# First MLP product by seven block products, with weight sums formed in SBUF by DVE and by transfers

## The chip, the cores and the metric

One core of one Trainium2 chip runs the whole kernel; there is one launch. The metric is the device time of that launch in microseconds, as the median of several executions. Lower is better.

## The reference, cut to what matters

One decoder layer on 256 tokens of width 2048, in fp32. The part that the change rewrites is the first MLP product; all else (attention heads, pooling, output projection, final norm) is computed as before.

```python
z = rmsnorm(h, norm2_w) @ mlp_w1          # [256, 2048] @ [2048, 8192]
h = h + jnp.square(jax.nn.relu(z)) @ mlp_w2   # [256, 8192] @ [8192, 2048]
h = rmsnorm(h, final_norm_w)
```

## The kernel before

Every product is made of matmuls on fp32r operands (a rounded fp32 form of TensorE). To keep fp32 accuracy an operand is split into a rounded part `hi` and a remainder `lo`, and three matmuls (hi·hi, hi·lo, lo·hi) stand for one product. The activations are split once and stay in SBUF. The weights are streamed: `wts` holds them as chunks of [128, 2048] floats (1 MB) in the order of their use. `raw_chunk` (L92) loads a chunk by a DMA on SP's queue into one of three `raw` buffers. `halves` (L99) splits it in two halves of 1024 columns: ScalarE copies to `hi` (L75), VectorE subtracts to `lo` (L76). There are four `hi` and four `lo` buffers, so splitting can run four halves ahead of TensorE and no further.

`as_chunk` (L208) multiplies one chunk with both token tiles (t = 0, 1, of 128 tokens): four k-tiles, two token tiles, three matmuls of 128x512, so 24 matmuls a chunk and 12 a half. After each half it calls `run_side`, which pops one piece of side work (transposes, evacuations) from the list `side` and issues it there.

The MLP runs in eight groups of 1024 hidden columns. `mlp1(g)` (L671) makes the hidden columns of group g: two strips of 512 columns, four chunks each, 192 matmuls; ScalarE and VectorE form relu² of them (L683, L685), and `back` transposes the result on TensorE (`turn4`, L635) and splits it into `z_hi`, `z_lo`. `mlp2(g)` (L697) multiplies these with the second weight matrix, 8 chunks and 192 matmuls, and `add_h` (L627) adds the sums to `h`. The loop runs `mlp1(g)` and then `mlp2(g - 1)` for g = 1 to 7; `mlp1(0)` stands ahead of it, and the second product of group 7 is the tail, one token tile after the other.

Ahead of `mlp1(0)`, the output projection (L651) fills `h`, and `make_u2` (L638) transposes it to `u2_hi`, `u2_lo`; these transposes wait in `side` and ride in the chunks that follow. The norm's factor is applied to the hidden columns, as a per-token scale (L683). The final norm's weights `fw` are loaded and scaled early (L611, L615).

A scheduler orders the instructions of every engine ahead of time; at run time each engine takes its queue strictly in order, and SP issues the loads in order.

Of the kernel before, what the change touches and what calls it, by code (L numbers as in the profile page):

```python
# [36 lines left out]
def hybrid_gla_pool_kernel(  # L37
# [17 lines left out]
    cp = ctx.enter_context(tc.tile_pool(name="cp", bufs=1))  # L55
    big = ctx.enter_context(tc.tile_pool(name="big", bufs=1))
# [4 lines left out]
    accp = ctx.enter_context(tc.tile_pool(name="accp", bufs=4, space=PSUM))  # L61
    gpp = ctx.enter_context(tc.tile_pool(name="gpp", bufs=4, space=PSUM))
    gt = ctx.enter_context(tc.tile_pool(name="gt", bufs=4))
    gstack = ctx.enter_context(ExitStack())
    gq = gstack.enter_context(tc.tile_pool(name="gq", bufs=1))

    def acc():
        return accp.tile([P, 512], F32, tag="acc", name="acc")
# [3 lines left out]

    # ---------------------------------------------------------------- weights
    def split(raw, hi, lo):
# [69 lines left out]

    # ------------------------------------------------------------- 1 / rms
    def rsqrt(dst, ssq, n, parts, w):
# [168 lines left out]

    # log gates over natural tokens (the factor 1/16 sits in the triangles)
    lgs = []
# [25 lines left out]

    # ke: meta tokens to their end, tile 0 to its end, the first chunk of each tile to its end
    def gates(h, t):
# [41 lines left out]

    # values
    vn = [gq.tile([P if t < 2 else META, H * DV], F32, tag=f"vn{t}", name=f"vn{t}") for t in range(3)]
# [22 lines left out]

    # queries
    qd = [gq.tile([P, S], F32, name=f"qd{h}") for h in range(H)]
# [83 lines left out]

    # output gate
    for s in range(2):  # L500
# [36 lines left out]

    # multi-scale pooling
    mo = []
# [53 lines left out]
    for g in range(4):  # L593
        p = ws_next(META - (2 << g))
        if g == 3:
            while side:
                side.pop(0)()
        side[1:1] = pooling(g, p)

    gstack.close()  # L600

    # ================================================================ phase 2
    lp = ctx.enter_context(tc.tile_pool(name="lp", bufs=1))
    zt = ctx.enter_context(tc.tile_pool(name="zt", bufs=3))
# [3 lines left out]
    fw = lp.tile([P, D], F32, name="fw")  # L608

    def load_fw():  # L610
        nc.sync.dma_start(out=fw, in_=rows[:, 768 : 768 + D].partition_broadcast(P))  # L611

    def scale_fw():
        # the last rsqrt leaves a factor -8192, a power of two
        dve.tensor_scalar(out=fw, in0=fw, scalar1=-1.0 / 8192.0, scalar2=None, op0=ALU.mult)  # L615

# [4 lines left out]
    rs3 = cp.tile([P, NT], F32, name="rs3")  # L621
    u2_hi = big.tile([P, KD, S], F32R, tag="u_hi", name="u2_hi")
    u2_lo = big.tile([P, KD, S], F32R, tag="u_lo", name="u2_lo")

# [13 lines left out]
    def make_u2(s, t):  # L638
        ps = turn4(h[:, t, s * 512 : (s + 1) * 512])
        ts = slice(t * P, (t + 1) * P)  # L640
        for j in range(4):
            k = 4 * s + j
            pj = ps[:, j * P : (j + 1) * P]
            act.activation(u2_hi[:, k, ts], pj, AF.Copy, scale=n2[:, k : k + 1])
            dve.scalar_tensor_tensor(
                out=u2_lo[:, k, ts], in0=pj, scalar=n2[:, k : k + 1],
                in1=u2_hi[:, k, ts].bitcast(F32), op0=ALU.mult, op1=ALU.subtract,
            )
# [17 lines left out]
    rsqrt(rs2, tot, D, P, NT)  # L666
    dve.tensor_tensor(out=rs2, in0=rs2, in1=rs2, op=ALU.mult)

    rz = {}

    def mlp1(g):  # L671
        nonlocal ci
        z_hi = mp.tile([P, 8, S], F32R, tag="m", name="z_hi")
        z_lo = mp.tile([P, 8, S], F32R, tag="m", name="z_lo")
        rz[g] = (z_hi, z_lo)
        for s in range(2):
            ps = [acc(), acc()]
            for c in range(4):
                as_chunk(ps, ci, u2_hi, u2_lo, 0, 4, 4 * c, c == 0, c == 3)
                ci += 1  # L680
            for t in range(NT):
                r = zt.tile([P, 512], F32, tag="r", name="r")
                act.activation(r, ps[t], AF.Relu, scale=rs2[:, t : t + 1])  # L683
                q = zt.tile([P, 512], F32, tag="q", name="q")
                dve.scalar_tensor_tensor(  # L685
                    out=q, in0=ps[t], scalar=0.0, in1=r, op0=ALU.max, op1=ALU.mult
                )


                def back(s=s, t=t, q=q):  # L690
                    pv = turn4(q).rearrange("p (j c) -> p j c", c=P)
                    ts = slice(t * P, (t + 1) * P)
                    evac_hl(z_hi[:, 4 * s : 4 * s + 4, ts], z_lo[:, 4 * s : 4 * s + 4, ts], pv)

                side.append(back)

    def mlp2(g):  # L697
        nonlocal ci
        z_hi, z_lo = rz.pop(g)
        for s in range(4):  # L700
            ps = [acc(), acc()]
            for c in range(2):
                as_chunk(ps, ci, z_hi, z_lo, 0, 4, 4 * c, c == 0, c == 1)
                ci += 1
            for t in range(NT):
                add_h(ps[t], t, s * 512, (s + 1) * 512)

    mlp1(0)
    side += [load_fw, idle, idle, idle, scale_fw]
    for g in range(1, GROUPS):  # L710
        mlp1(g)
        mlp2(g - 1)
    # ======================================= last group: one token tile after the other
    z_hi, z_lo = rz.pop(GROUPS - 1)
    e_hi = big.tile([P, KD, S], F32R, tag="u_hi", name="e_hi").rearrange("p k c -> p (k c)")
    e_lo = big.tile([P, KD, S], F32R, tag="u_lo", name="e_lo").rearrange("p k c -> p (k c)")
# [34 lines left out]
    for s in range(4):  # L751
        ws = []
        for c in range(2):
            raw = raw_chunk(ci)
            ci += 1
            if s == 2:
                for hf in range(2):
                    o = c * 2048 + hf * 1024
                    hi, lo = e_hi[:, o : o + 1024], e_lo[:, o : o + 1024]
# [29 lines left out]
def _weights(np, w_in, w_out, w1, w2):  # L789
    """All weights as one run of chunks [128, 2048], in the order in which they are used."""  # L790
    def ws(a):  # [2048, n*256] -> n strips of two chunks, each 8 k-tiles of 256 columns
        n = a.shape[1] // 256
        b = a.reshape(2, 8, P, n, 256).transpose(3, 0, 2, 1, 4)
        return b.reshape(n * 2, P, 2048)

    def st(a):  # [512*c, n*512] -> [n, c] chunks, each 4 k-tiles of 512 columns
        c, n = a.shape[0] // 512, a.shape[1] // 512
        b = a.reshape(c, 4, P, n, 512).transpose(3, 0, 2, 1, 4)
        return b.reshape(n, c, P, 2048)
# [16 lines left out]
    for g in range(1, GROUPS):  # L816
        m1(g)
        m2(g - 1)
# [58 lines left out]
```

## Time and profile before

| | |
|---|---|
| median of 3 runs (lowest, highest) | 1049.33 us (1048.45, 1050.74) |
| span of the profiled execution | 1046.9 us |
| TensorE matmuls busy | 1035.2 us, 99% of the span |
| VectorE (DVE) busy | 605.9 us, 58% |
| ScalarE (ACT) busy | 480.6 us, 46% |
| GpSimd (POOL) busy | 0.2 us |
| moved by DMA | 197.15 MB, 188 GB/s over the span |
| granted TensorE clock, mean | 0.997 |

The profile shows one execution. Its page gives the span, from the first instruction to the last, and no further time of that execution; the median of the runs lies 2.4 us above the span. Engine times overlap, so they do not add up. The rows that the prediction uses stand in groups below.

### The profile page before, as it was taken

The page shows a single profiled execution, that of the slowest core. Times are in us where ns is not written, and L with a number is a line of the kernel's source. Part 1 is how long each engine was busy: PE and PEld are TensorE (multiplying, and loading weights), DVE is VectorE, ACT ScalarE, POOL GpSimd, SP SyncE. Part 2 cuts the span into 40 slices and gives each one's busy share as a digit, 9 for nine tenths or more (in the row PEclk, how much of TensorE's full clock was granted, in tenths as well). Part 3 has the DMA queues.
Part 4 walks back from the last instruction along what each step waited for, and adds up shares of the span by engine and source line. Part 5 has one row for each costly group of instructions (what it writes and reads, how often), then busy time and mean ns, then how long its engine had stood idle before and what let it go on. Part 6 is the DMA issues. An engine that isn't in the chain of part 4 may idle for free.

```text
span 1046.9 us, 12935 instructions
## 1 busy us (share of the span) xinstructions
PE 1035.2 (99%) x5237; PEld 877.2 (84%) x5237; DVE 605.9 (58%) x773; ACT 480.6 (46%) x630; POOL 0.2 (0%) x4
## 2 busy tenths in 40 slices
PE   8999999999999999999999999999999999999996
PEld 7989878998888888888888888888888888888885
DVE  7555544876666555555555555565555555555574
ACT  6537544444555444434434433443443344344351
POOL 0000000000000000000000000000000000000000
PEclk9999999999999999999999999999999999999998
DMA  9663434447554545555555555555555555545542
GB/s 348 241 239 137 161 124 159 146 155 288 186 190 172 201 173 189 198 184 182 201 189 179 196 194 184 185 200 186 182 197 191 185 188 199 185 178 201 188 174 81
DMA packets 29820, 197.15 MB, mean 188 GB/s; under 512 B 3456, under 2 KB 3968, under 8 KB 6704
## 3 DMA queue, kind: packets, MB, share of 16 engines
q1 hardware_dynamic: 29760, 196.32, 52.9%
q8 instruction: 41, 0.67, 0.3%
q14 instruction: 19, 0.16, 0.0%
HBM read 194.21 MB, written 2.10 MB: 188 GB/s over the span
## 4 chain that ended last, share of the span: by engine, by line
PE 98%; DMA 1%; SPq 0%; DVE 0%; ACT 0%; issue 0%; ACTq 0%
PE acc L217 25%; PE acc L219 25%; PE acc L218 25%; PE acc L202 4%; PE acc L203 4%; PE acc L204 4%; PE gp L635 2%; PE acc L777 1%; PE acc L776 1%; PE acc L778 1%; DMA raw<-in_wts 1%; PE acc L256 1%; PE acc L258 1%; PE acc L257 1%; PE gp L472 0%; PE gp L473 0%
## 5 line engine op out<-in xcount | busy, mean ns | idle before, releaser
L76 DVE TENSOR_TENSOR lo<-raw,hi 128x1024 fp32r<-128x1024 f32 (+1 forms) x356 | 425.8, 1200 | 373.6 <-ACT hi L75 373.3
L75 ACT CAST hi<-raw 128x1024 fp32r<-128x1024 f32 (+1 forms) x356 | 366.1, 1033 | 484.2 <-PE acc L219 409.4
L217 PE MATMUL acc<-hi,u_hi 128*128 128x512 f32 x576 | 228.5, 397 | 0.0
L219 PE MATMUL acc<-hi,u_lo 128*128 128x512 f32 x576 | 224.8, 390 | 0.0
L218 PE MATMUL acc<-lo,u_hi 128*128 128x512 f32 x576 | 224.5, 390 | 0.0
L217 PE MATMUL acc<-hi,z_hi 128*128 128x512 f32 x448 | 175.7, 392 | 0.0
L219 PE MATMUL acc<-hi,z_lo 128*128 128x512 f32 x448 | 174.5, 389 | 0.0
L218 PE MATMUL acc<-lo,z_hi 128*128 128x512 f32 x448 | 174.4, 389 | 0.0
L219 PEld LDWEIGHTS acc<-hi,u_lo 128*128 128x128 f32 x576 | 108.1, 188 | 23.0
L217 PEld LDWEIGHTS acc<-hi,u_hi 128*128 128x128 f32 x576 | 108.2, 188 | 22.0
L218 PEld LDWEIGHTS acc<-lo,u_hi 128*128 128x128 f32 x576 | 108.3, 188 | 21.7
L219 PEld LDWEIGHTS acc<-hi,z_lo 128*128 128x128 f32 x448 | 84.1, 188 | 17.7
L217 PEld LDWEIGHTS acc<-hi,z_hi 128*128 128x128 f32 x448 | 84.1, 188 | 17.1
L218 PEld LDWEIGHTS acc<-lo,z_hi 128*128 128x128 f32 x448 | 84.2, 188 | 17.0
L202 PE MATMUL acc<-u_hi,hi 128*128 128x272 f32 (+4 forms) x320 | 92.7, 290 | 0.0
L203 PE MATMUL acc<-u_lo,hi 128*128 128x272 f32 (+4 forms) x320 | 91.4, 286 | 0.0
L204 PE MATMUL acc<-u_hi,lo 128*128 128x272 f32 (+4 forms) x320 | 91.2, 285 | 0.0
L202 PEld LDWEIGHTS acc<-u_hi,hi 128*128 128x128 f32 x320 | 60.3, 189 | 1.0 <-issue 0.8
L203 PEld LDWEIGHTS acc<-u_lo,hi 128*128 128x128 f32 x320 | 60.2, 188 | 0.1
L204 PEld LDWEIGHTS acc<-u_hi,lo 128*128 128x128 f32 x320 | 60.1, 188 | 0.0
L627 DVE TENSOR_TENSOR h<-acc,h 128x512 f32<-128x512 f32 (+1 forms) x71 | 45.6, 679 | 5.2 <-PE acc L778 5.2
L683 ACT ACTIVATE r<-acc,rs 128x512 f32<-128x512 f32 x32 | 21.9, 690 | 15.7 <-PE acc L219 15.7
(189 smaller groups left out, 841.6 us busy)
## 6 DMA issues: line engine op xcount, KB each, us to landing
raw<-in_wts SPq DMA_DIRECT2D x175, 1024.0 KB, 4.8
xn<-in_x SPq DMA_DIRECT2D x2, 1024.0 KB, 11.8
h<-in_x SPq DMA_DIRECT2D x2, 1024.0 KB, 6.7
out<-h SPq DMA_DIRECT2D x8, 256.0 KB, 2.9
xTs<-in_xT SPq DMA_DIRECT2D x3, 546.0 KB, 9.7
pw<-in_pool_w SPq DMA_DIRECT2D x4, 256.0 KB, 5.1
fw<-in_rows SPq DMA_DIRECT2D x1, 1024.0 KB, 7.7
raw<-in_wts SPq DMA_DIRECT2D x2, 256.0 KB, 3.5
```

The costliest lines, as they stand in the source:

```text
L75: act.copy(out=hi, in_=raw)
L76: dve.tensor_tensor(out=lo, in0=raw, in1=hi.bitcast(F32), op=ALU.subtract)
L202: pe.matmul(o, hi[:, cs], u_hi[:, k, lo_t:L], start=k == 0, stop=False)
L203: pe.matmul(o, hi[:, cs], u_lo[:, k, lo_t:L], start=False, stop=False)
L204: pe.matmul(o, lo[:, cs], u_hi[:, k, lo_t:L], start=False, stop=k == KD - 1)
L217: pe.matmul(ps[t], a_hi[:, k, ts], hi[:, cs], start=st, stop=False)
L218: pe.matmul(ps[t], a_hi[:, k, ts], lo[:, cs], start=False, stop=False)
L219: pe.matmul(ps[t], a_lo[:, k, ts], hi[:, cs], start=False, stop=sp)
L256: pe.matmul(o, hi[:, cs], u_hi[:, k, :], start=k == 0, stop=False)
L627: dve.tensor_tensor(out=hs, in0=p, in1=hs, op=ALU.add)
L635: pe.transpose(ps[:, j * P : (j + 1) * P], src[:, j * P : (j + 1) * P], ident)
L683: act.activation(r, ps[t], AF.Relu, scale=rs2[:, t : t + 1])
```

## The change

The first product of groups 1 to 7 is computed block by block. For a group, the token tiles (2) times the two halves of the 2048 input channels (2) form four activation blocks, and the input halves times the two strips of 512 columns form four weight blocks. Seven products of sums of such blocks (a Strassen form) replace eight plain block products. Each of the seven is one token tile wide: `product` makes 24 matmuls of 128x512 on two chunks.

- The seven activation operands are made once, during `mlp1(0)`, by `prepare`: the norm's factor is multiplied in (`rms2_rows`, `norm_a`), blocks are added or subtracted (`combine`), and each operand is split to `ah`, `al` and kept in SBUF (pool `asp`).
- The weight sums are made for each group in place. A group loads eight chunks of the first matrix: x (2 chunks), z (2), y (2), v (2). x is used plain in product 1; then `add_load` adds the z block to it by a DMA from GpSimd's queue that accumulates in SBUF, and product 5 uses the sum. The same way y is added to the z tiles, for product 7. `add_raw` adds y and later v to the x tiles on VectorE (128x2048), for products 6 and 4. The chunks of z and y that `add_load` reads come from HBM a second time.
- The chunks of `mlp2(g - 1)` alternate with the products, one `half(j)` of 24 matmuls after each product or so.
- PSUM sums of the products are kept (`keep`, a copy on ScalarE) and combined in `hidden`; relu and square are two ScalarE steps.
- Buffers: four `raw` buffers, and four more of the same size (`xy`), which first hold `u2`. PSUM pools are cut anew after `mlp1(0)`. The side list is emptied ahead of `mlp1(0)`. `fw` is loaded and scaled at the start of the tail. A smaller SBUF area is reserved for GpSimd's DMA descriptors.

```diff
-    rawp = ctx.enter_context(tc.tile_pool(name="rawp", bufs=3))
+    rawp = ctx.enter_context(tc.tile_pool(name="rawp", bufs=4))
...
     rsqrt(rs2, tot, D, P, NT)
...
+    while side:
+        side.pop(0)()
+    gstack.close()
+    asp = ctx.enter_context(tc.tile_pool(name="asp", bufs=1))
...
+    def norm_a(kh):
+        a = mp.tile([P, 8, S], F32, tag="m", name="a")
+        full.append(a)
+        u_h, u_l = (u.bitcast(F32) for u in u2[kh])
+        dve.tensor_tensor(out=a, in0=u_h, in1=u_l, op=ALU.add)
+        dve.tensor_tensor(out=a, in0=a, in1=rb2.unsqueeze(1).to_broadcast([P, 8, S]), op=ALU.mult)
...
+    def operand(i, t, kh, sign=1.0):
+        a = blk(t, kh)
+        hi, lo = (asp.tile([P, 8, P], F32R, name=f"{n}{i}") for n in ("ah", "al"))
+        if sign > 0:
+            act.copy(out=hi, in_=a)
+            dve.tensor_tensor(out=lo, in0=a, in1=hi.bitcast(F32), op=ALU.subtract)
...
+        return [
+            rms2_rows, lambda: norm_a(0), lambda: operand(1, 0, 0), lambda: norm_a(1),
+            lambda: operand(2, 0, 1), s5, s7, s6, s3,
+        ]
...
+    def product(i, ps, raws, start):
+        a_hi, a_lo = ops_a[i]
+        for c in range(2):
+            for hf, (hi, lo) in enumerate(halves(raws[c])):
+                for j in range(2):
+                    k = c * 4 + hf * 2 + j
+                    cs = slice(j * 512, (j + 1) * 512)
+                    kw = dict(skip_group_check=True)
+                    pe.matmul(ps, a_hi[:, k], hi[:, cs], start=start and k == 0, stop=False, **kw)
+                    pe.matmul(ps, a_hi[:, k], lo[:, cs], start=False, stop=False, **kw)
+                    pe.matmul(ps, a_lo[:, k], hi[:, cs], start=False, stop=k == 7, **kw)
+            run_side()
+
+    def add_raw(dst, src):
+        dve.tensor_tensor(out=dst, in0=dst, in1=src, op=ALU.add)
+
+    def add_load(dst, c):
+        nc.gpsimd.dma_start(out=dst, in_=wts[c], accum_op=ALU.add)
...
+        xs = [xy_load(base), xy_load(base + 1)]
+        zs = [xy_load(base + 2), xy_load(base + 3)]
+        product(1, b_a, xs, True)
+        x1 = keep(b_a, "x1")
+        for i in range(2):
+            add_load(xs[i], base + 2 + i)
+        half(0)
+        ys = [raw_chunk(base + 4), raw_chunk(base + 5)]
+        for i in range(2):
+            add_load(zs[i], base + 4 + i)
+        product(5, b_d, xs, True)
+        x5 = keep(b_d, "x5")
+        add_raw(xs[0], ys[0])
+        half(1)
+        add_raw(xs[1], ys[1])
+        product(3, b_d, ys, False)
+        half(2)
+        half(3)
+        product(6, b_a, xs, False)
+        x2 = keep(b_a, "x2")
+        hidden(g, 1, 0, b_d, x2, -1.0)
+        vs = [raw_chunk(base + 6), raw_chunk(base + 7)]
+        add_raw(xs[0], vs[0])
+        half(4)
+        add_raw(xs[1], vs[1])
+        product(7, b_a, zs, False)
+        hidden(g, 1, 1, b_a, x5, -1.0)
+        half(5)
+        product(4, b_a, xs, False)
+        hidden(g, 0, 1, b_a, None, 1.0)
+        half(6)
+        product(2, b_b, vs, True)
+        hidden(g, 0, 0, b_b, x1, 1.0)
+        half(7)
...
+    fw = mp.tile([P, D], F32, tag="m", name="fw")
+    nc.sync.dma_start(out=fw, in_=rows[:, 768 : 768 + D].partition_broadcast(P))
+
+    dve.tensor_scalar(out=fw, in0=fw, scalar1=-1.0 / 8192.0, scalar2=None, op0=ALU.mult)
```

Two places show how the order of the engines' queues changes. A row of an order is: line, operation, written tile <- read tiles, shape, and in brackets the semaphores that it waits for (DMAHW for SP's transfers, DMASW for GpSimd's).

VectorE's queue in the middle of a group, before: `lo` is a split, `h` the add of a finished strip, `z_lo` the evacuation of a transpose.

```order
L76 TENSOR_TENSOR lo_4378<-raw_4375,hi_4377 128x1024 [waits DMAHW5_49,Activation_49]
L685 SCALAR_TENSOR_TENSOR q_4319<-acc_4179,r_4317 128x512 [waits Activation_49]
L685 SCALAR_TENSOR_TENSOR q_4323<-acc_4180,r_4321 128x512 [waits Activation_49]
L76 TENSOR_TENSOR lo_4382<-raw_4375,hi_4381 128x1024 [waits PE_49,Activation_49]
L76 TENSOR_TENSOR lo_4412<-raw_4409,hi_4411 128x1024 [waits DMAHW6_49,Activation_49]
L497 TENSOR_TENSOR z_lo_4178<-gp_4349,z_hi_4177 128x4x128 [waits Activation_49]
L76 TENSOR_TENSOR lo_4416<-raw_4409,hi_4415 128x1024 [waits Activation_49]
```

The same queue now, from the end of product 1 to the first split of half(1) and on; `blk_4940` and `blk_4942` are the two x chunks, `raw_5028` and `raw_5030` the two y chunks.

```order
L621 TENSOR_TENSOR h_2510<-acc_4804,h_2510 128x512 [waits PE_49]
L621 TENSOR_TENSOR h_2510<-acc_4805,h_2510 128x512 [waits PE_49]
L77 TENSOR_TENSOR lo_4973<-blk_4942,hi_4972 128x1024 [waits DVE_49,Activation_49]
L77 TENSOR_TENSOR lo_4997<-raw_4994,hi_4996 128x1024 [waits DMAHW3_49,DVE_49,Activation_49]
L77 TENSOR_TENSOR lo_5001<-raw_4994,hi_5000 128x1024 [waits Activation_49]
L77 TENSOR_TENSOR lo_5035<-blk_4940,hi_5034 128x1024 [waits DMASW2_49,Activation_49]
L77 TENSOR_TENSOR lo_5039<-blk_4940,hi_5038 128x1024 [waits PE_49,Activation_49]
L784 TENSOR_TENSOR blk_4940<-blk_4940,raw_5028 128x2048 [waits DMAHW4_49,DVE_49]
L77 TENSOR_TENSOR lo_5055<-blk_4942,hi_5054 128x1024 [waits DMASW3_49,Activation_49]
L77 TENSOR_TENSOR lo_5059<-blk_4942,hi_5058 128x1024 [waits Activation_49]
L784 TENSOR_TENSOR blk_4942<-blk_4942,raw_5030 128x2048 [waits DMAHW5_49,DVE_49]
L77 TENSOR_TENSOR lo_5080<-raw_5077,hi_5079 128x1024 [waits DMAHW6_49,Activation_49]
```

Two splits wait for GpSimd's transfers (DMASW2, DMASW3), and two adds of 128x2048 stand among the splits.

TensorE's queue where `mlp1(0)` begins, before: `u2` is the transposed `h`, `gp<-cst,h` one block of four transposes of `make_u2`.

```order
L217 MATMUL acc_3220<-hi_3223,u2_hi_2511 128x512
L218 MATMUL acc_3220<-lo_3224,u2_hi_2511 128x512
L219 MATMUL acc_3220<-hi_3223,u2_lo_2512 128x512
L635 MATMUL gp_3243<-cst_85,h_2502 128x128 [waits DVE_49]
L217 MATMUL acc_3219<-hi_3227,u2_hi_2511 128x512 [waits Activation_49]
```

The same place now.

```order
L220 MATMUL acc_3041<-hi_3176,mo_lo_2116 128x512
L218 MATMUL acc_3260<-hi_3264,u2_2518 128x512 [waits Activation_49]
L219 MATMUL acc_3260<-lo_3265,u2_2518 128x512 [waits DVE_49]
L629 MATMUL gp_3228<-cst_85,h_2510 128x128 [waits DVE_49]
L220 MATMUL acc_3260<-hi_3264,u2_2519 128x512
L629 MATMUL gp_3241<-cst_85,h_2510 128x128 [waits DVE_49]
L218 MATMUL acc_3261<-hi_3264,u2_2518 128x512
```

The last transposes of `h` stood after the first half chunk (12 matmuls) and now stand after two matmuls.

## Rows read from the trace of the kernel before

**Rows 1.** The page: busy us, share of the span, instructions of each engine.
```profile
PE 1035.2 (99%) x5237; PEld 877.2 (84%) x5237; DVE 605.9 (58%) x773; ACT 480.6 (46%) x630; POOL 0.2 (0%) x4
```
**Rows 2.** The page: the chain that ended last, shares by engine.
```profile
PE 98%; DMA 1%; SPq 0%; DVE 0%; ACT 0%; issue 0%; ACTq 0%
```
**Rows 3.** Stretches of one group each: length, busy per engine, clock, DMA, GB/s.
```profile
662.93:751.90 88.97, 88.97 (x402) 73.66 (x401) 49.14 (x49) 38.18 (x40) 0.00 (x0) 1.00 0.55 190
751.90:840.87 88.97, 88.97 (x402) 73.66 (x401) 49.13 (x49) 38.18 (x40) 0.00 (x0) 1.00 0.54 189
```
**Rows 4.** Timeline of TensorE in a group: start us, duration us, instruction.
```profile
639.63 0.39 PE L217 MATMUL acc<-hi,u_hi 128*128 128x512 f32 x1
639.86 0.39 PE L218 MATMUL acc<-lo,u_hi 128*128 128x512 f32 x1
...
642.36 0.39 PE L217 MATMUL acc<-hi,u_hi 128*128 128x512 f32 x1
```
**Rows 5.** Waits: engine, line, waited for: us in total, times, longest.
```profile
ACT hi L75 <- PE acc L219: 409.4, 251, 2.7
DVE lo L76 <- ACT hi L75: 373.3, 308, 2.7
```
**Rows 6.** Groups by line and shape: count, busy us, mean ns, idle before.
```profile
L76 DVE TENSOR_TENSOR lo<-raw,hi 128x1024 fp32r<-128x1024 f32 x340 | 415.7, 1224 | 370.8 <-ACT hi L75 370.6
L75 ACT CAST hi<-raw 128x1024 fp32r<-128x1024 f32 x340 | 357.1, 1052 | 481.6 <-PE acc L219 409.4 <-PE acc L203 55.0 <-issue 13.4
L685 DVE SCALAR_TENSOR_TENSOR q<-acc,r 128x512 f32<-128x512 f32 x32 | 21.9, 691 | 7.2 <-ACT r L683 7.2
L683 ACT ACTIVATE r<-acc,rs 128x512 f32<-128x512 f32 x32 | 21.9, 690 | 15.7 <-PE acc L219 15.7
L630 ACT ACTIVATE junk<-h 128x512 f32<-128x512 f32 x14 | 8.7, 626 | 8.8 <-DVE h L627 8.8
L76 DVE TENSOR_TENSOR lg<-lg 128x1536 fp32r<-128x1536 f32 x1 | 1.8, 1758 | 0.4 <-ACT lg L75 0.4
L615 DVE TENSOR_SCALAR fw<-fw 128x2048 f32<-128x2048 f32 x1 | 1.2, 1222 | 0.0
```
**Rows 7.** Timeline of VectorE in the tail, where it runs without a pause.
```profile
1002.30 1.23 DVE L76 TENSOR_TENSOR lo<-raw,hi 128x1024 fp32r<-128x1024 f32 x1 [0.32 <-ACT hi L75]
1003.44 1.22 DVE L76 TENSOR_TENSOR e_lo<-raw,e_hi 128x1024 fp32r<-128x1024 f32 x1
1004.58 1.22 DVE L76 TENSOR_TENSOR lo<-raw,hi 128x1024 fp32r<-128x1024 f32 x1
```
**Rows 8.** Timeline of VectorE at the end of the output projection.
```profile
301.96 1.28 DVE L627 TENSOR_TENSOR h<-acc,h 128x512 f32<-128x512 f32 x2
```
**Rows 9.** DMA issues: tile<-tensor, queue, count, KB each, median us to landing.
```profile
raw<-in_wts SPq DMA_DIRECT2D x175, 1024.0 KB, 4.8
xn<-in_x SPq DMA_DIRECT2D x2, 1024.0 KB, 11.8
fw<-in_rows SPq DMA_DIRECT2D x1, 1024.0 KB, 7.7
```
**Rows 10.** The first loads and the last stretch, columns as in rows 3.
```profile
5.00:15.00 10.00, 8.52 (x60) 7.77 (x59) 6.83 (x14) 6.89 (x14) 0.00 (x0) 1.00 1.00 395
...
1030.00:1047.00 17.00, 8.16 (x59) 7.57 (x57) 7.41 (x26) 3.91 (x8) 0.00 (x0) 0.80 0.34 123
```
**Rows 11.** The chain in order of time: where the last `h` transposes ran.
```profile
305.10 0.44 PE gp L635 x4
308.29 0.44 PE gp L635 x4
```

More of the change, by code (lines that the diff above doesn't have):

```diff
@@ L697, in mlp2 @@
[L697 to L709, printed above, removed]
+    rs2q = cp.tile([P, NT], F32, name="rs2q")
+    dve.tensor_tensor(out=rs2q, in0=rs2, in1=rs2, op=ALU.mult)
@@ new lines, in hybrid_gla_pool_kernel, with rms2_rows @@
+    rb2 = cp.tile([P, S], F32, name="rb2")
+    while side:
+        side.pop(0)()
+    gstack.close()
+    asp = ctx.enter_context(tc.tile_pool(name="asp", bufs=1))
+    def rms2_rows():
+        ps = gp()
+        for t in range(NT):
+            dg = zt.tile([P, P], F32, tag="q", name="dg2")
+            dve.tensor_scalar(out=dg, in0=ident, scalar1=rs2[:, t : t + 1], scalar2=None, op0=ALU.mult)
+            pe.matmul(ps[:, t * P : (t + 1) * P], cst[:, C_ONE : C_ONE + P], dg, start=True, stop=True)
+        dve.tensor_copy(out=rb2, in_=ps[:, :S])
@@ new lines, in combine, with prepare, s5, s7 @@
+    def combine(dst, x0, x1, op):
+        dve.tensor_tensor(out=blk(*dst), in0=blk(*x0), in1=blk(*x1), op=op)
+    def prepare():
+        def s5():
+            operand(4, 1, 1)
+            combine((1, 1), (1, 1), (1, 0), ALU.subtract)
+            operand(5, 1, 1)
+        def s7():
+            combine((1, 0), (0, 0), (1, 0), ALU.subtract)
+            operand(7, 1, 0)
+        def s6():
+            combine((0, 0), (0, 0), (1, 1), ALU.add)
+            operand(6, 0, 0, -1.0)
+        def s3():
+            combine((0, 1), (0, 0), (0, 1), ALU.subtract)
+            operand(3, 0, 1)
+        return [
+            rms2_rows, lambda: norm_a(0), lambda: operand(1, 0, 0), lambda: norm_a(1),
+            lambda: operand(2, 0, 1), s5, s7, s6, s3,
+        ]
@@ new lines, in hybrid_gla_pool_kernel, with z_pair, z_back, back @@
+    rz = {}
+    def z_pair():
+        return [mp.tile([P, 8, S], F32R, tag="m", name=n) for n in ("z_hi", "z_lo")]
+    def z_back(g, s, t, q):
+        def back():
+            z_hi, z_lo = rz[g]
+            pv = turn4(q).rearrange("p (j c) -> p j c", c=P)
+            ts = slice(t * P, (t + 1) * P)
+            evac_hl(z_hi[:, 4 * s : 4 * s + 4, ts], z_lo[:, 4 * s : 4 * s + 4, ts], pv)
+        return back
+    side += [idle] + prepare()
+    rz[0] = z_pair()
+    for s in range(2):
+        ps = [acc(), acc()]
+        for c in range(4):
+            as_chunk(ps, ci, u2[c // 2][0], u2[c // 2][1], 0, 4, 4 * (c % 2), c == 0, c == 3)
+            ci += 1
+        for t in range(NT):
+            r = zt.tile([P, 512], F32, tag="r", name="r")
+            act.activation(r, ps[t], AF.Relu, scale=rs2q[:, t : t + 1])
+            q = zt.tile([P, 512], F32, tag="q", name="q")
+            dve.scalar_tensor_tensor(out=q, in0=ps[t], scalar=0.0, in1=r, op0=ALU.max, op1=ALU.mult)
+            side.insert(t, z_back(0, s, t, q))
@@ new lines, in hybrid_gla_pool_kernel, with xy_load @@
+    banks.close()
+    accp = ctx.enter_context(tc.tile_pool(name="pair", bufs=3, space=PSUM))
+    gpp = ctx.enter_context(tc.tile_pool(name="turn", bufs=2, space=PSUM))
+    sump = ctx.enter_context(tc.tile_pool(name="sum", bufs=1, space=PSUM))
+    def xy_load(c):
+        raw = xy.tile([P, 2048], F32, tag="xy", name="blk")
+        nc.sync.dma_start(out=raw, in_=wts[c])
+        return raw
+    def product(i, ps, raws, start):
[10 more added lines that the diff above has]
+            run_side()
@@ new lines, in add_raw, with keep, hidden @@
+    def add_raw(dst, src):
+        dve.tensor_tensor(out=dst, in0=dst, in1=src, op=ALU.add)
+    def add_load(dst, c):
+        nc.gpsimd.dma_start(out=dst, in_=wts[c], accum_op=ALU.add)
+    def keep(ps, name):
+        x = zt.tile([P, 512], F32, tag=name, name=name, bufs=1)
+        act.copy(out=x, in_=ps)
+        return x
+    def hidden(g, s, t, ps, x, sign):
+        q = zt.tile([P, 512], F32, tag="q", name="q")
+        if x is None:
+            r = ps
+        else:
+            r = zt.tile([P, 512], F32, tag="r", name="r")
+            dve.tensor_tensor(out=r, in0=ps, in1=x, op=ALU.add)
+        act.activation(q, r, AF.Relu, scale=sign)
+        act.activation(q, q, AF.Square)
+        side.append(z_back(g, s, t, q))
@@ new lines, in group, with half @@
+    def group(g):
+        nonlocal ci
+        base = ci
+        ci += 16
+        rz[g] = z_pair()
+        z_hi, z_lo = rz[g - 1]
+        pair = []
+        def half(j):
+            if j % 2 == 0:
+                pair[:] = [acc(), acc()]
+            as_chunk(pair, base + 8 + j, z_hi, z_lo, 0, 4, 4 * (j % 2), j % 2 == 0, j % 2 == 1)
+            if j % 2:
+                for t in range(NT):
+                    add_h(pair[t], t, j // 2 * 512, (j // 2 + 1) * 512)
+        b_a, b_d, b_b = (sump.tile([P, 512], F32, tag=n, name=n) for n in ("sa", "sd", "sb"))
+        xs = [xy_load(base), xy_load(base + 1)]
[32 more added lines that the diff above has]
+        half(7)
+        del rz[g - 1]
@@ L710, in hybrid_gla_pool_kernel @@
     for g in range(1, GROUPS):
[L711 to L712 removed]
+        group(g)
+    while side:
+        side.pop(0)()
     z_hi, z_lo = rz.pop(GROUPS - 1)
[L715 to L716 removed]
+    e = [[xy.tile([P, 2048], F32R, tag="xy", name="e") for _ in range(2)] for _ in range(2)]
+    fw = mp.tile([P, D], F32, tag="m", name="fw")
+    nc.sync.dma_start(out=fw, in_=rows[:, 768 : 768 + D].partition_broadcast(P))
```

69 lines of the change are left out of this document (26 added, 43 removed).

## The prediction

> **What bounds the kernel now.** I read the page first: matmuls fill 99% of the span, VectorE 58%, ScalarE 46% [rows 1]. The chain that ended last agrees: 98% of it is TensorE [rows 2]. A mean over stages can hide a local limit, so I read two groups of the MLP apart: each takes 88.97 us, TensorE is busy for all of it at a clock of 1.00, VectorE for 49.1, ScalarE for 38.2, the DMA engines for 0.55 [rows 3]. The waits tell who waits for whom: the copies to `hi` stand 409 us behind TensorE (they want a buffer back), the subtractions 373 us behind the copies [rows 5]. So splitting runs as far ahead as four buffers let it, and TensorE waits for nobody. A matmul less is time off the end, as long as nothing else comes late.
>
> **The change, part by part.**
>
> *(a) Matmuls removed.* Starts of twelve matmuls lie 2.73 us apart [rows 4], so one costs 0.227 us; the 0.39 us of a row is latency that overlaps. Seven products of 24 stand for 192 matmuls: 24 fewer a group, 5.44 us, and in seven groups 38.1 us. A group falls from 88.97 to 83.53 us of TensorE work. This is on the path, to the full.
>
> *(b) Work added to VectorE and ScalarE in a group.* A product takes two chunks and gives 24 matmuls, where one chunk gave 24. So seven products split 14 chunks where eight were split: 12 more half-splits. A split shows as 1.22 us [rows 6], but back to back they start 1.14 us apart [rows 7]: 13.7 us. Four adds of 128x2048: no such operation is in the trace; the nearest is the subtraction of 128x1536 with 1.758 us, and from 1024 to 1536 columns it grew by 0.534 us, so 2048 would take 2.29, and 2.2 back to back: 8.8 us. Bounds are 1.22 (the multiply of `fw`, 128x2048 with a single tensor operand) and two splits, 2.45 [rows 6]; I take 2.2, since two tensors are read here as in the split. The combination in `hidden` costs VectorE about what `q` cost (four of 0.69 us [rows 6]), less one, which combines nothing. Together 49.1 + 13.7 + 8.8 - 0.7 = 70.9 of 83.5 us, 85%. ScalarE gets 12 copies of 1.05 us (12.6), three `keep` and four further squares at about 0.6 (bounds 0.626 and 0.690 [rows 6]): 38.2 + 12.6 + 4.2 = 55 us. Neither is the bound in sum. During a product, though, 2.72 us of matmuls pay for a chunk's two splits, 2.28 us, and an add of 2.2 can only be paid for by a neighbouring `half`. Hidden, but with little cover.
>
> *(c) The adding transfers, the term that decides.* The last split of product 1 (`lo_4973`) must have read the second x chunk before the transfer may add to it, and product 5 begins one `half` later. Let T0 be the start of product 1 on TensorE. With four buffers, split n can start when TensorE is done with split n-4, so that last split waits for the first six matmuls or so at most: what is before it in VectorE's queue are the two adds to `h` of the half before, a pair in 1.28 us [rows 8]. T0 + 0.2 + 1.28 + 1.14 = T0 + 2.7: the transfer starts. Back from the other end: product 1, half(0) and product 5 are 5.44 us each, so half(1) wants its first split at T0 + 16.3. Between the landing and that moment VectorE's queue must get through a copy on ScalarE (1.05), two splits (2.3), the add of y (2.2) and half(1)'s own split (1.14), with 0.3 of handing over: 7.0 us. So the transfer must land by T0 + 9.3, a window of 6.6 us from issue. Behind the waiting split on VectorE stand both adds of y and all splits of half(1), so every microsecond over the window stops TensorE for one, and costs 7 us over the groups. The first x chunk has a window of some 11 us, and the z chunks are added 20 us before product 7 wants them: those wait for nobody.
>
> How long does the landing take? No transfer of the trace adds, and none starts from GpSimd's queue. A plain chunk of 1 MB lands 4.8 us after its issue (median of 175), the slowest rows are 7.7 for `fw` and 11.8 for `xn`, with other loads around them [rows 9]. 4.8 gives no stall; 11.8 gives 5.2 a group, 36 us. Between them: at a DMA share of 1.00 the engines moved 395 GB/s [rows 10], so 1.05 MB is 2.65 us of all engines. If an addition moves twice the bytes, 4.8 + 2.65 = 7.45. In the same window SP issues the raw loads of y, and the first x chunk's own addition is under way; one of these sharing the engines adds up to 2.65 more, 10.1. I take the middle, 8.8: a stall of 2.1 to 2.2 us, in seven groups 15 us. Estimates all; both ends stay for the range (0 to 36).
>
> The Trainium skill ("Collectives: The Full Stack", section "The bandwidth ceiling: the fold count and why AG ≠ RS ≠ AR") says that a transfer which adds is slower not for the addition but for its second source read, and gives a ratio of 1.93 measured in rings of cores. By it alone, an estimate, the landing is 4.8 + 0.93 x 2.65 = 7.3 us, the stall 0.7 a group, and the sum comes out some 10 us lower than mine. No row here shows an adding transfer, so the trace neither bears this out nor speaks against it.
>
> In all, a group loads 16 MB and adds 4 MB more of transfers: 190 GB/s [rows 3] become about 250, below the 395 seen. Loads of SP are issued early; the z and y additions on GpSimd's queue stand ahead of the next group's x ones, but come due earlier. No cost.
>
> *(d) Transposes of the hidden columns* come behind an add, two ScalarE steps and a transfer to `side` instead of one and one; I give them 0.4 us a group of waiting, a transpose block's own time (0.44 [rows 11]) as the bound: 3 us.
>
> *(e) The stage of `mlp1(0)`.* The last transposes of `h` ran at 305.10 and 308.29 [rows 11], one half chunk or more after the adds to `h`. Now they stand after two matmuls, and wait for these adds: 0.7 to 1.3 us [rows 8]. Then `prepare` puts about 21 us of VectorE work (four adds or multiplies of 2.2, eleven smaller of 1.14) into a stage of 192 matmuls, 43.5 us, where the splits take 18: near 90% with what else is there, and a few splits come late by a microsecond or two (the fourth chunk, the first of the second strip). I take 5 us, range 2 to 8.
>
> *(f) The tail.* `fw` is loaded only after half(7) and lands 7.7 us later [rows 9]; its multiply of 1.22 us [rows 6] stands in VectorE's queue ahead of splits of the tail. Four halves, 10.9 us of matmuls, lie split ahead. I take 2 us, range 0 to 5. Phase one (pooling and heads) is left as it was.
>
> Sum: -38.1 + 15 + 3 + 5 + 2 = -13. The profiled span, 1046.9 us, becomes about 1033.5; the median of the runs lies 2.4 above the span, so **1036 us**.
>
> **The rivals.**
>
> *The transfer is hidden.* If it lands in 6.6 us or less, term (c) is zero: 1036 - 15 = 1021; with VectorE's slack a little better than I think, 1016, and worse, 1026. For it: 4.8 us for plain chunks, the DMA engines half idle [rows 3, 9]. Against it: none of those 4.8 us waits for a second read.
>
> *Slower: the transfer takes too long.* The break-even is a stall of 13 + 15 = 28 us in seven groups, 4.0 each, a landing of 10.7 us. A transfer that adds and lands in 14 us stalls TensorE 7.4 us in each group, 52 us: 1073. `xn` with 11.8 us shows that 1 MB can take this long [rows 9], 5.2 a group, 1057. And TensorE that pauses may also lose its clock: in the last stretch, where it worked 8.2 of 17 us, the granted clock was 0.80 [rows 10], a mean of the 2.4 GHz level and the 1.2 GHz one; with that a stall of 4 us weighs more than 4. Against it: `xn` was read amid a queue of first loads at a DMA share of 1.00 [rows 10], and a group has about half of that.
>
> *The saving is hidden anyway, by VectorE.* If an add costs two splits and a bit (2.45 and handing over), a group's VectorE sum is 72 of 83.5 us; for it to bind in sum it would need 12 us more. So this comes only locally, as 1 or 2 us at each of the four adds, 28 to 56 us in seven groups: with (c) at zero 1049 to 1077, about the same or slower. The rows of splits, back to back at 1.14 us [rows 7], speak against it.
>
> **How the numbers follow.** The forecast (some stall, 1024 to 1044) has a chance of 0.41; the hidden transfer (1012 to 1024) 0.29; about the same, in a band of 2 us on either side of 1049.3, which is what a measurement can tell, 0.06; slower 0.24, of it 0.18 by the transfer and 0.06 by VectorE at the adds. Faster is 0.41 + 0.29 = 0.70. The range of 8 in 10 leaves out the best end of the hidden case and the slow landings above 11 us or so: 1016 to 1058.
>
> **What would show it.** Matmuls 168 fewer, with products at 0.227 us a matmul, show (a). The rows of DMA issues give the landing of L787's transfers: near 8.8, or below 6.6, or above 10.7. TensorE's idle time ahead of product 5 and of half(1), released by a GpSimd transfer or by a VectorE split behind one, shows (c); the same idle time released by VectorE at products 6 and 4, where no adding transfer is due, would show the VectorE rival instead. A group of 83.5 us means no stall, 86 the forecast, over 89 the slower rival. The start of `mlp1(0)` should show idle time of TensorE around `turn4`, the tail a split behind `fw`. The forecast is wrong if idle time in a group is under 0.5 us, or if it stands at units that have no sum to wait for.

## The result

The changed kernel took 1077.7 us (median of four runs, 1075.6 to 1079.9) beside 1050.0 for the kernel before (median of four; the three runs ahead of the prediction gave 1049.33); the ratio of their runs is 1.0268, with a 95% interval of 1.025 to 1.0286. It is slower by 28 us, where 1036 us was forecast and the range ended at 1058. The profiled execution has a span of 1078.2 us, against 1046.9.

The profile page of the changed kernel, engines, DMA queues and chain, beside [rows 1, 2]:

```profile
PE 1029.0 (95%) x5073; PEld 856.9 (79%) x5073; DVE 777.9 (72%) x896; ACT 597.5 (55%) x770; POOL 24.6 (2%) x32
...
q1 hardware_dynamic: 29760, 196.32, 49.0%
q0 software_dynamic: 4032, 29.36, 13.2%
...
PE 80%; DMA 11%; DVE 4%; issue 2%; ACT 2%; SPq 0%; ACTq 0%; POOL 0%; POOLq 0%
PE acc L218 13%; PE acc L220 13%; PE acc L219 13%; DMA blk<-in_wts 10%; PE acc L203 4%; PE acc L204 4%; PE acc L205 4%; PE sa L778 3%; PE sa L780 3%; PE sa L779 3%; PE sd L779 3%; DVE lo L77 2%; PE sd L780 2%; PE sd L778 2%; PE gp L629 2%
...
raw<-in_wts SPq DMA_DIRECT2D x147, 1024.0 KB, 4.8
blk<-in_wts SPq DMA_DIRECT2D x28, 1024.0 KB, 4.8
blk<-in_wts POOLq DMA_DIRECT2D x28, 1024.0 KB, 12.7
```

TensorE was 98% of the chain before and is 80% now. A new link holds 10%, over 100 us: transfers into `blk`, the x and z chunks. The last lines price it. In the median a plain chunk still lands after 4.8 us, an adding transfer after 12.7 (28 of them, 10.8 to 15.6).

Stretches of the changed kernel, columns as in [rows 3] (length, then TensorE, weight loads, VectorE, ScalarE, GpSimd, clock, DMA share, GB/s); the first is one whole group, the second part of it:

```profile
563.00:656.00 93.00, 88.40 (x378) 71.02 (x377) 70.92 (x64) 53.88 (x60) 3.46 (x4) 0.96 0.70 226
...
543.00:577.00 34.00, 31.85 (x139) 25.52 (x138) 21.27 (x21) 17.72 (x21) 2.60 (x3) 0.97 1.02 300
```

A group takes 93 us, where 89 was the old length and 83.5 was expected without stalls. VectorE's 70.9 us is what the prediction worked out. The mean DMA share of 0.70 looks harmless, but for 34 us around the group's start the engines are full: a share of 1.02. Plain loads feel it too: one that SP issues at 554.78 lands only at 572.57, after 17.8 us.

The chain of waits through one product 5, in order of time (start, length, what), from the last split of product 1:

```profile
562.41 1.24 DVE lo L77
...
563.99 15.62 DMA blk<-in_wts
...
579.71 1.05 ACT hi L76
...
580.79 1.24 DVE lo L77
...
582.07 0.79 PE sd L779
```

The transfer that was given 8.8 us took 15.6. The timeline of TensorE in the same place (start, length, instruction, in brackets its idle time and what ended it):

```profile
571.78 0.39 PE L220 MATMUL acc<-hi,z_lo 128*128 128x512 f32 x1
573.52 0.51 PE L778 MATMUL sd<-hi,ah 128*128 128x512 f32 x1 [1.35 <-ACT hi L76]
574.78 0.50 PE L779 MATMUL sd<-lo,ah 128*128 128x512 f32 x1 [0.76 <-DVE lo L77]
...
577.15 0.63 PE L779 MATMUL sd<-lo,ah 128*128 128x512 f32 x1
577.58 0.63 PE L780 MATMUL sd<-hi,al 128*128 128x512 f32 x1
...
580.81 0.49 PE L778 MATMUL sd<-hi,ah 128*128 128x512 f32 x1 [1.66 <-ACT hi L76]
582.07 0.79 PE L779 MATMUL sd<-lo,ah 128*128 128x512 f32 x1 [0.77 <-DVE lo L77]
```

TensorE ends half(0) at 572.0 and begins half(1) at 586.3: product 5 takes 14.3 us where its matmuls need 5.44, a stall of 8.85. It pauses four times: from one start to the next, less a matmul's 0.23, that is 1.5, 1.0, 1.8 and 1.0 us, 5.4 together (the brackets, which are taken from the modelled ends, give 4.5). Behind the pauses matmuls start 0.43 us apart and not 0.227, the 1.2 GHz level in place of 2.4, and that is the other 3.4 us. The clock granted from 575.2 to 578.4 and from 582.6 to 585.4 was 0.50, and 1.00 before the pauses and after them.

### The profile page after: what moved, and what is told of

The parts are those of the page before. It is cut to its first block, busy times and chain, and to the rows that moved or that the text cites. A ratio compares the mean times of both kernels' runs of the same rounds, so it can differ in the third digit from the quotient of the medians.

```text
span 1078.2 us, 13027 instructions
## 1 busy us (share of the span) xinstructions
PE 1029.0 (95%) x5073; PEld 856.9 (79%) x5073; DVE 777.9 (72%) x896; ACT 597.5 (55%) x770; POOL 24.6 (2%) x32
## 3 DMA queue, kind: packets, MB, share of 16 engines
q0 software_dynamic: 4032, 29.36, 13.2%
## 4 chain that ended last, share of the span: by engine, by line
PE 80%; DMA 11%; DVE 4%; issue 2%; ACT 2%; SPq 0%; ACTq 0%; POOL 0%; POOLq 0%
PE acc L218 13%; PE acc L220 13%; PE acc L219 13%; DMA blk<-in_wts 10%; PE acc L203 4%; PE acc L204 4%; PE acc L205 4%; PE sa L778 3%; PE sa L780 3%; PE sa L779 3%; PE sd L779 3%; DVE lo L77 2%; PE sd L780 2%; PE sd L778 2%; PE gp L629 2%
## 5 line engine op out<-in xcount | busy, mean ns | idle before, releaser
L77 DVE TENSOR_TENSOR lo<-raw,hi 128x1024 fp32r<-128x1024 f32 (+1 forms) x300 | 355.1, 1195 | 131.1 <-ACT hi L76 119.6
L76 ACT CAST hi<-raw 128x1024 fp32r<-128x1024 f32 (+1 forms) x300 | 306.8, 1030 | 216.5 <-PE acc L220 100.4
L77 DVE TENSOR_TENSOR lo<-blk,hi 128x1024 fp32r<-128x1024 f32 x140 | 169.3, 1222 | 110.1 <-ACT hi L76 108.3
L76 ACT CAST hi<-blk 128x1024 fp32r<-128x1024 f32 x140 | 146.4, 1051 | 164.1 <-DMA blk<-in_wts 81.1
L778 PE MATMUL sa<-hi,ah 128*128 128x512 f32 x224 | 87.3, 390 | 0.0
L780 PE MATMUL sa<-hi,al 128*128 128x512 f32 x224 | 87.2, 389 | 0.0
L779 PE MATMUL sa<-lo,ah 128*128 128x512 f32 x224 | 87.1, 389 | 0.0
L778 PE MATMUL sd<-hi,ah 128*128 128x512 f32 x112 | 51.9, 463 | 25.8 <-ACT hi L76 25.7
L784 DVE TENSOR_TENSOR blk<-blk,raw 128x2048 f32<-128x2048 f32 x28 | 64.1, 2290 | 0.7
L779 PE MATMUL sd<-lo,ah 128*128 128x512 f32 x112 | 52.7, 470 | 7.7 <-DVE lo L77 7.6
## 6 DMA issues: line engine op xcount, KB each, us to landing
blk<-in_wts POOLq DMA_DIRECT2D x28, 1024.0 KB, 12.7
```

Source lines behind the costliest of these rows:

```text
L76: act.copy(out=hi, in_=raw)
L77: dve.tensor_tensor(out=lo, in0=raw, in1=hi.bitcast(F32), op=ALU.subtract)
L778: pe.matmul(ps, a_hi[:, k], hi[:, cs], start=start and k == 0, stop=False, **kw)
L779: pe.matmul(ps, a_hi[:, k], lo[:, cs], start=False, stop=False, **kw)
L780: pe.matmul(ps, a_lo[:, k], hi[:, cs], start=False, stop=k == 7, **kw)
L784: dve.tensor_tensor(out=dst, in0=dst, in1=src, op=ALU.add)
```

## The experiments

Two explanations of the late landing had to be told apart. Theory 1: the 16 engines are full, since an adding transfer holds them about twice as long as a plain one and four come in one burst with the ordinary loads. Theory 2: a transfer of GpSimd's queue, or an adding one, is late by itself. A rival to both: VectorE is late and the transfer only looks guilty.

### What the rest of the change is worth

```diff
-        for i in range(2):
-            add_load(xs[i], base + 2 + i)
...
-        for i in range(2):
-            add_load(zs[i], base + 4 + i)
```

> All four adding transfers of a group are left out (the sums z + x and y + z are missing, so products 5 and 7 work on other data). It prices everything of the change but the transfers. If the adding transfers cause the loss, by whatever mechanism, product 5 falls from 14.3 us to its 5.44 us of matmuls, a group from 93 to about 84, and the time to about 1020 us (1050 - 38 + 8 for the start, the tail and the transposes). If VectorE's load (70.9 us in a group) causes it, a group stays above 89 and the time above 1045 us.

Measured 1021.07 us (ratio 0.9733, 0.9719 to 0.9748), a span of 1018.3. All other work stands, and TensorE no longer waits at product 5, which takes 5.44 us in all seven groups. One group:

```profile
554.60:639.00 84.40, 84.34 (x378) 68.86 (x377) 70.96 (x64) 54.28 (x59) 0.00 (x0) 1.00 0.54 200
```

VectorE does the same 71 us of work in it. So the rest of the change gives 28.6 us of span back, and the adding transfers cost all that was lost: 1078.2 - 1018.3 = 59.9 us, 8.6 a group. VectorE's load as the cause is out.

### Adding or the queue

```diff
-        nc.gpsimd.dma_start(out=dst, in_=wts[c], accum_op=ALU.add)
+        nc.gpsimd.dma_start(out=dst, in_=wts[c])
```

> The same 28 transfers at the same places of GpSimd's queue, but they overwrite and do not add (the sums are missing; all orders of the queues are those of the changed kernel). Theory 1, the engines: an adding transfer takes 5.06 us of all 16 engines, a plain one about 2.65, so the burst before product 5 shrinks by 10 us, the landing falls from 12.7 to about 7 us, a group to 84-86 us and the time to 1020-1035 us. Theory 2, the queue: a transfer of GpSimd's queue is late whatever it does; the landing stays above 10 us and the time above 1060 us.

Measured 1025.41 us (0.977, 0.9756 to 0.9785). The queues of its DMA view, and its issues:

```profile
q1 hardware_dynamic: 29760, 196.32, 51.2%
q0 software_dynamic: 4032, 29.36, 7.8%
...
blk<-in_wts POOLq DMA_DIRECT2D x28, 1024.0 KB, 7.0
```

The same 4032 packets and 29.36 MB held the engines for 7.8% of 1023.2 us, 2.85 us a transfer; when they add, 13.2% of 1078.2 us, 5.08 each. The factor is 1.78; in the runs with fewer or later additions, below, an adding transfer held them for 5.5 us, a factor of 1.9. The landing falls from 12.7 to 7.0 us. The 28 transfers as plain copies thus cost 4 us of the whole time (1025.4 beside 1021.1), nearly all of them in the first group or ahead of it, and land after 7.0 us, at the least 5.0, where SP's chunks take 4.8. The other 52 us come with the addition. These are the numbers of theory 1 (about 7 us, 1020 to 1035) and not those of theory 2.

The Trainium skill ("Collectives: The Full Stack", section "The bandwidth ceiling: the fold count and why AG ≠ RS ≠ AR") says of rings of cores that the transfer which adds is slower for its second source read, with a ratio of 1.93. For this local addition the runs show 1.78 to 1.9 in engine time, near that ratio; no run here shows the reads themselves.

### Fewer adding transfers

```diff
-        for i in range(2):
-            add_load(zs[i], base + 4 + i)
```

> The two additions to the z chunks are left out (product 7 works on z alone), the two to the x chunks stay. Theory 1 (shared engines, full from 543 to 577 us in the trace): 10 us of engine time less in the burst, the landing of the x additions falls from 14-15.6 to about 10, the group to 86-88 and the time to about 1030-1045 us. Theory 2 (an adding transfer is slow by itself): landing still 12 us or more, the time within 8 us of 1078.

Measured 1040.52 us (0.9923, 0.9907 to 0.994). The landing of the x additions fell to 8.5 us in the median. Its chain of waits at the same place:

```profile
557.09 9.39 DMA blk<-in_wts
...
566.58 1.06 ACT hi L76
...
567.67 1.24 DVE lo L77
```

The second x transfer lands after 9.4 us, not 15.6, though it is the same instruction on the same queue. What went is two z additions that nobody was waiting for. Theory 2 alone cannot give that. The time is also near what the prediction's window makes of it. In this group the landing is 2.9 us over (T0 + 12.2, where T0 + 9.3 was the limit), and in all seven some 24 us; the span is 20.3 above that of the kernel without additions. The sum hides an uneven split: in the first group the second x addition takes 14.6 us with no z addition near it and costs about 7 us, in the other six 8.4 to 9.8 and some 2 us each. In the first group the plain loads of its own z chunks run at that time, and the DMA share from 372 to 393 is 0.99.

### The same transfers, later

The z additions stay, but each is made to depend on the landed x chunk by an operation of one column on VectorE.

```diff
+        product(5, b_d, xs, True)
+        for z in zs:
+            dve.scalar_tensor_tensor(
+                out=z[:, 0:1], in0=xs[1][:, 0:1], scalar=0.0, in1=z[:, 0:1], op0=ALU.mult, op1=ALU.add
+            )
         for i in range(2):
             add_load(zs[i], base + 4 + i)
-        product(5, b_d, xs, True)
```

> All four adding transfers of a group stay, but the two to the z chunks start only after the two to the x chunks have landed (two operations of one column on VectorE make them depend on it). The result is whole. Theory 1 (shared engines; the z additions stood 8 and 18 us ahead of the x ones and took 10 us of engine time from them): the x additions land in 8.5-10 us as without the z ones, the group is 86-88 us, the time 1035-1048. Theory 2 (what counts is the number of adding transfers on the queue, not when they run): the time stays above 1065.

Measured 1048.63 us (1.0001, 0.9991 to 1.0011): 29 us faster than the changed kernel with the same work, just off the upper end expected. The second x addition lands after 8.4 to 9.9 us in six groups, and after 14.2 in the first. Where the changed kernel issues GpSimd's transfers in one group (the first two are the z ones, the wait of the last two is for splits of x):

```profile
540.20 0.88 POOL L787 DMA_DIRECT2D blk<-in_wts  x1 [67.87 <-DMA blk<-in_wts]
550.38 0.86 POOL L787 DMA_DIRECT2D blk<-in_wts  x1 [9.30 <-DMA blk<-in_wts]
558.21 0.86 POOL L787 DMA_DIRECT2D blk<-in_wts  x1 [6.97 <-DVE lo L77]
563.99 0.86 POOL L787 DMA_DIRECT2D blk<-in_wts  x1 [4.92 <-DVE lo L77]
```

In this group the second z addition had landed (562.99) a microsecond before the second x addition was issued. What it left in the way was a backlog: two plain loads that had shared the engines with it landed only at 565.15 and 572.57. The order alone is worth half of the loss. VectorE in the experiment shows why it is 8 us behind the one without z additions:

```profile
568.49 0.23 DVE L834 SCALAR_TENSOR_TENSOR blk<-blk 128x1 f32<-128x1 f32 x2 [3.45 <-DMA blk<-in_wts]
568.64 2.28 DVE L784 TENSOR_TENSOR blk<-blk,raw 128x2048 f32<-128x2048 f32 x1
570.84 2.35 DVE L77 TENSOR_TENSOR lo<-blk,hi 128x1024 fp32r<-128x1024 f32 x2
```

The small operations wait for the second x chunk, and the first add of y, which without them runs during that wait, now stands behind them: the split of the second chunk begins 2.35 us after the landing's release and not 1.2, a little over 1 us in each group.

### A wider window

```diff
+        half(1)
         product(5, b_d, xs, True)
         x5 = keep(b_d, "x5")
         add_raw(xs[0], ys[0])
-        half(1)
         add_raw(xs[1], ys[1])
+        half(2)
         product(3, b_d, ys, False)
-        half(2)
```

> half(1) runs ahead of product 5 and half(2) ahead of product 3, so 5.44 us more lie between the issue of the x additions and product 5; all transfers stay. The result is whole. Theory 1 in the form that the landing, not the count of operations, sets the end: the landing stays at 14-15.6 us, but the window grows from 6.6 to 12.1, so 3 us of waiting remain where there were 5.4 plus 3.4 of slow clock: 1030-1050 us. If the transfers come later in turn because more loads now stand before them, the time stays above 1065.

Measured 1067.0 us (1.0178, 1.0163 to 1.0193), outside what the first form expected and within the second. Its chain of waits in a group and TensorE's timeline:

```profile
551.85 19.07 DMA raw<-in_wts
```

```profile
572.11 0.50 PE L218 MATMUL acc<-hi,z_hi 128*128 128x512 f32 x1 [2.89 <-ACT hi L76]
573.38 0.80 PE L219 MATMUL acc<-lo,z_hi 128*128 128x512 f32 x1 [0.76 <-DVE lo L77]
```

Product 5 no longer waits. half(1) does, for a plain load, which took 19 us instead of 4.8. The load in the same place of SP's order took 17.8 us in the changed kernel, but there half(1) came later and did not wait for it. So a plain load on SP's queue is late in the burst as well: that fits theory 1 and not a lateness of GpSimd's queue or of adding transfers alone.

### The clock after the pauses

Twelve matmuls more ahead of product 5 and fourteen between its chunks; `fill` writes a sum that nobody reads.

```diff
+        fill(12, b_d, z_hi)
-        product(5, b_d, xs, True)
+        product(5, b_d, xs, True, (b_b, z_hi))
```

> The changed kernel with 26 matmuls of 128x512 more in each group, on data that is there, whose sums nobody reads: 12 ahead of product 5 and 14 between its two chunks, where TensorE waits. They cost 26 x 0.227 = 5.9 us a group, 41 us in all, if nothing else gave way. If the pauses alone make the loss (5.4 us a group), they fill the pauses and the time stays at 1075-1082. If the lower clock after the pauses makes 3.4 us of each group's loss, TensorE does not pause and keeps its clock: a group of 90 us, the time 1053-1063, faster with more work.

Measured 1074.59 us (1.025, 1.0235 to 1.0265). The mean clock rose from 0.974 to 0.998, and 182 more matmuls, 41 us of TensorE's time, fitted into a kernel that got 3 us faster. That is 0.4 us under the first range expected and far from the second: the clock is not where most of the loss lies. TensorE's timeline says what took its place:

```profile
569.36 2.88 PE L772 MATMUL sd<-z_hi,ah 128*128 128x512 f32 x12
574.80 3.33 PE L772 MATMUL sb<-z_hi,ah 128*128 128x512 f32 x14
582.50 0.50 PE L219 MATMUL acc<-lo,z_hi 128*128 128x512 f32 x1 [1.41 <-DVE lo L77]
```

At full clock product 5 ends sooner, and half(1) then waits for its split, which stands on VectorE behind the add that waits for the landing. The landing sets the end by that way too; the slow matmuls lay nearly all in time that would have passed anyway.

### The sums on VectorE

First z + x alone, from the z chunk that already lies in SBUF; then all four sums.

```diff
         for i in range(2):
-            add_load(xs[i], base + 2 + i)
+            add_raw(xs[i], zs[i])
```

> The sum z + x is made by VectorE from the z chunk that already lies in SBUF (two more adds of 2.29 us in a group, 75.5 us of VectorE); the sum y + z stays with the adding transfers, which have 20 us of time. The result is whole. If only the landing before product 5 is at fault, the stall goes: a group of 84-86 us and 1020-1035 us. If VectorE around product 5 has no room for 4.6 us more, TensorE waits there for splits: a group of 87-90 us, 1040-1060 us.

Measured 1019.69 us (0.9721, 0.9707 to 0.9736). It is 58 us faster than the changed kernel, and as fast as the one without any sum by a transfer (1021.07): the additions to z, still adding transfers that land after 9.2 us in the median, cost nothing that shows when nobody near waits.

```diff
         for i in range(2):
-            add_load(zs[i], base + 4 + i)
+            add_raw(zs[i], ys[i])
```

> All four sums of a group by VectorE, no adding transfer, 4 MB less loaded in a group. The result is whole. VectorE has 70.9 + 4 x 2.29 = 80.1 us of a group's 84. If the adds fit between the splits, 1018-1024 us as with x alone (1019.7); if VectorE's cover is gone, product 7 and what is near waits for splits: 1025-1045 us.

Measured 1048.88 us (1.0002, 0.9992 to 1.0012): a little beyond the 1045 expected: with four sums VectorE's cover is gone. A stretch of about one group, and TensorE at the start of product 5:

```profile
548.00:636.00 88.00, 85.74 (x382) 69.40 (x381) 79.14 (x69) 54.92 (x60) 0.00 (x0) 1.00 0.54 195
```

```profile
568.14 0.50 PE L779 MATMUL sd<-lo,ah 128*128 128x512 f32 x1 [1.96 <-DVE lo L77]
```

VectorE is busy for 79 of 88 us, TensorE waits for a split, and a group is 3 to 4 us longer than with two sums, where it took 84.1 (the first one 6 us longer). So the transfers had a reason; two of the four were one place too close to their use.

### A version that beats both

On top of z + x by VectorE, `prepare` is cut into smaller steps, so that splits stand between them, and the operands of products 3, 7 and 6 are made last.

```diff
+            rms2_rows, lambda: half_a(0), lambda: half_b(0), lambda: operand(1, 0, 0),
+            lambda: half_a(1), lambda: half_b(1), lambda: operand(2, 0, 1), lambda: operand(4, 1, 1), s5,
+            lambda: combine((1, 0), (0, 0), (1, 0), ALU.subtract), s3, lambda: operand(3, 0, 1),
+            lambda: operand(7, 1, 0), lambda: operand(6, 0, 0, -1.0),
...
-    side += [idle] + prepare()
+    side += prepare()
```

> As e4 (z + x by VectorE, y + z by adding transfers), and the steps of prepare are cut finer, so that VectorE's splits stand between them and the last three operands come at the end of mlp1(0) or in group 1. The result is whole. In e4 the split at 353.53 us stands behind 4.5 us of other VectorE work and TensorE waits 2.6 us for it, with 1.5 us more at the lower clock. If the order of VectorE's queue is what is late there, 3-4 us go: 1015-1018. If VectorE's sum in this stage is the limit, the wait only moves: 1019-1021.

Measured 1016.38 us (0.9692, 0.9678 to 0.9705). The version without the finer steps ran beside it:

> e4_x_dve once more, beside e9_even on the same chip, since the two are apart by less than 0.5%: 1019-1021 us.

Measured 1020.41 us (0.9727, 0.9713 to 0.974), so the finer steps and the new order together give 4.0. The stage of `mlp1(0)` in the version without and in this one, in stretches as above:

```profile
325.50:374.90 49.40, 46.81 (x210) 38.38 (x208) 44.60 (x60) 28.91 (x40) 0.00 (x0) 0.97 0.50 190
```

```profile
325.50:374.00 48.50, 48.50 (x225) 40.00 (x224) 47.19 (x63) 32.23 (x44) 0.00 (x0) 1.00 0.58 213
```

In the first TensorE pauses for 2.6 us, and the clock is 0.97; in the second it is busy throughout, and since product 1 of the next group begins at 370.56 there (374.86 in the first), the stage itself is 4.3 us shorter. VectorE is busier in the second, so its order was late, not its sum. Which of the two changes gave more was not tried.

## Why the prediction was wrong

By its own steps:

- **(a) Matmuls removed: right.** The MLP's products have 168 matmuls fewer (PE in all 5073 where there were 5237, since four small ones are new), and products at full clock run at 0.227 us a matmul. The kernel without additions confirms the gain.
- **(b) VectorE and ScalarE: right.** 70.9 and 53.9 us a group were measured, 70.9 and 55 worked out; the add of 128x2048 takes 2.29 us, as the line through two shorter rows gave. That this cover is thin, and lost at 80 us, is what the run with four sums shows.
- **(c) The adding transfers: the window right, the landing wrong.** The issue came 2.9 us after product 1's start (2.7 forecast). From the landing at 579.61 to half(1) passed 6.7 us (7.0 forecast). The landing should have been there at T0 + 9.3 and came at T0 + 18.5, 9.2 us over, for a stall of 8.85. In the seven groups the landing was 7.5 to 9.2 us over and the stall 6.8 to 9.4: that each microsecond over the window costs one held to the end. The term that was mis-sized is the landing, 8.8 us forecast and 13.4 to 15.6 measured for the second x chunk, and so the stall, 15 us forecast and 58 measured in product 5 over the seven groups.

  Two choices made it. "The z chunks are added 20 us before product 7 wants them: those wait for nobody" was true and beside the point: nobody waits for them, but they hold the engines for 10 us just ahead of the x additions and leave the loads of SP late, as the runs without them (landing 8.5) and with them later showed. The same with "No cost", which rested on a mean of about 250 GB/s. And of what stands in the window I let one plain megabyte, 2.65 us, share the engines; there were the first x addition, which landed only at T0 + 11.2, and three loads of SP, two of them held up since before, all in a stretch of full engines. The addition itself was sized well: twice the time of a plain megabyte was taken, 1.78 to 1.9 times was measured; without the z ones the second x addition took 8.4 to 9.8 us in six groups, where 8.8 was forecast. The first group, 14.6 us there, is not explained by the z additions.
- **(d) Transposes: right in size.** Without the stall a group takes 84.1 us with z + x on VectorE and 84.35 without any addition, 0.6 to 0.8 over its matmuls, 4 to 6 us in all (3 forecast). That it is the transposes which make it is not shown.
- **(e) `mlp1(0)`: right in size, in part by luck.** The last relu of its second strip ran at 369.91 before and at 375.80 in the changed kernel; less the 0.8 by which the stage began later, 5 us, as forecast, and 4 of them went by a finer order. Of its two parts only one came: a split on VectorE late by 2.6 us at 355.99, with slow matmuls behind it. The wait of the last transposes of `h` did not show: they start at 326.26, 0.27 us after the matmul ahead of them. [rows 11] was misread there, for it shows the transposes of an earlier strip; the last ones of the kernel before ran at 327.66 and 330.86.
- **(f) The tail: over-sized.** From its first products to the end it is 52.9 us, 52.7 before; the 2 us for `fw` did not come. It landed after 4.7 us, and its multiply at 1030.20 stood where splits lay ahead.

Without (c) the sum was -28; the kernel without additions shows -28.6, with (d) some 2 us over and (f) 2 us under, which cancel by luck. The slower rival described the right place, mechanism and even price (14 us of landing gave 1073), but the transfer got a chance of 0.18 of being slow because of its "against": that a group uses half of the DMA engines. That is a mean over 89 us. I had written that a mean can hide a local limit and read TensorE by it, and did not ask it of the DMA engines: 4 adding transfers of 5.1 us and six plain loads of 2.7 take about 36 us of full engines, most of it in the 34 us around a group's start. The remark that slow clock would add to the stall held for the rows but not for the time.

The least landings fit the engine times: 7.6 us for an adding transfer and 5.0 for a plain one of the same queue, each some 2 us above the 5.5 and 2.85 us for which it held the engines. What stays open is why an addition holds them longer, and why that was 5.1 us in the runs with a full burst and 5.5 in the others.

## What to carry to other kernels

Price a transfer by the time that it holds the engines, and lay all transfers of a stage, those that nobody waits for included, into the stretch in which they will really run; a mean share below 1 is no cover for a burst. Where two kinds of transfers share the engines, put the one with the shorter deadline first; widening its window moves the wait to the next load. If one engine is near its limit and a queue is too, divide the work between them: two sums each were worth 29 us over four on VectorE and 58 over four by transfers. Such a mix was tried in one form alone, z + x on VectorE.

## What the runs showed of the hardware

An addition in the transfer held the DMA engines 1.78 times as long as the same bytes copied (5.08 us and 2.85 a megabyte chunk; 5.5 in the runs with fewer or later additions), and issuing one kept GpSimd busy for 0.86 us. In the burst plain loads of SP's queue, 4.8 us in the median, took up to 20.6 us in the changed kernel. After pauses of 1 to 2 us TensorE's matmuls started 0.43 us apart, at a granted clock of 0.50, for some 3 us before they came back to 0.227; with the pauses filled by idle matmuls the mean clock went from 0.974 to 0.998, though this gave only 3 us.
